# Crossing from one token tile to the next at the junctions of a two-layer trunk, and 13 adaLN steps moved into its first turns

## The chip, the cores and the metric

The kernel runs on one core of one Trainium2 chip. The metric is the device time of one execution in microseconds (us). Engines: PE (TensorE, matmuls), DVE (VectorE), ACT (ScalarE), POOL (GpSimd), SP (SyncE, which here only issues DMAs).

## The reference

Two layers act on 256 tokens of width 2048, in float32. Each layer is a token mixer and an MLP, both between norms that a conditioning vector modulates (adaLN):

```python
def reference(x, c, ...):
    cs = jax.nn.silu(c)
    for l in range(DEPTH):
        mod = (cs @ ada_w[l] + ada_b[l])[:, None, :]
        sh_a, sc_a, g_a, sh_m, sc_m, g_m = jnp.split(mod, 6, axis=-1)
        h = rms_norm(x, norm_g[l, 0]) * (1.0 + sc_a) + sh_a
        o = fox_sb_mixer(h, ...) if l % 2 == 0 else dsa_mixer(h, ...)
        x = x + g_a * rms_norm(o @ mix_w_out[l], norm_g[l, 1])
        h = rms_norm(x, norm_g[l, 2]) * (1.0 + sc_m) + sh_m
        y = jnp.square(jax.nn.relu(h @ ff_w1[l])) @ ff_w2[l]
        x = x + g_m * rms_norm(y, norm_g[l, 3])
    return x
```

`ada_w` is [2, 2048, 12288], `ff_w1` [2, 2048, 8192], `mix_w_out` [2, 2048, 2048]. A next norm needs a whole row of x, and that needs a whole row of the product before it: between `o @ mix_w_out` and `h @ ff_w1`, and between the MLP and the next layer's mixer, nothing of the next product can begin until every column of the last one is there.

## The kernel before, in words

**Tokens.** The 256 tokens are two tiles of 128 (t = 0, 1). X holds the residual, Y the branch, HT the normed and modulated activations, transposed, as two parts (high and low) of a split product.

**Weights.** Every weight matrix is cut into strips of columns and each strip into slots along the contraction. `order` lists all slots. A slot's weights are split on chip: ACT makes the high part (`wh`, L1261), DVE the low part (`wl`, L1265), `AHEAD` = 3 slots ahead of PE (`convert(s, 0)` and `convert(s, 1)`). There are four buffers each for `wh` and `wl`, so a conversion waits until PE is through with the slot four before. In each slot `mm_slot` issues the matmuls. In a "wmov" strip (both out-projections, the second MLP product, the mixer inputs) the weight moves and the tokens stand: three products per k and tile (L728 to L730). In a "wide" strip (the first MLP product) the weights stand and both tiles move: 512 columns of HT high and low together (L738) and 256 with `wl` (L740).

**Evictions.** At a strip's end its `evac` goes to `posts`; each slot runs one stage of it. `junction` is what stands behind the last strip of out_proj(0), MLP(0) and out_proj(1): it drains the posts, makes the statistics of both tiles together (`rstd_next`, with a power on POOL), writes the two diagonals DG (L420), transposes X by DG into HT two columns of 128 at a time (`ht_pair`: matmuls at L426, scale and shift on ACT at L437 and once on DVE at L435, cast L440, difference L441), and updates X (L467). The remaining pairs follow in `next_ht`, one pair per slot of the next strip. J1, J2 and J3 stand for these three junctions below.

**adaLN.** The product of silu(c) with `ada_w` runs on DVE in steps (`ada_step`, L296) of one [128, 1024] tile each, 512 KB by DMA through SP's queue; 16 steps make a job. Shift and scale of layer 0's first norm are wanted at once and come in 64 finer "parts" (`part_step`, L366) during four "turns" (the slots up to `phase_ends`: 3, 16, 32, 48), in which the first six weight units are multiplied by as much of HT as is there; HF holds HT's float copy. Later steps are paid from a balance, `owed`, that grows with each slot; a step is issued when it reaches 1. `attention_gate(0)`, called at slot GJ = 7 of the third strip of out_proj(0), first issues whatever steps are missing up to number 96 and then multiplies the gate into GG by a matmul with ones (L218).

The code stands in program order on every engine: no engine overtakes itself.

## Time and profile before

| | us |
|---|---|
| median of three runs | 2296.44 |
| the runs | 2292.89, 2296.44, 2297.43 |
| the profiled execution, whole | 2295.47 |
| its span, first to last instruction | 2293.6 |
| PE busy in the span | 2190.8 |
| DVE busy | 1684.9 |
| ACT busy | 1129.3 |
| mean granted clock of PE, as a share of full | 0.985 |

The profile is one execution; its times are read against its own 2295.47 us, of which 1.9 us lie outside the span. A row of a timeline says when an instruction (or a run of like ones) starts, how long it takes, on which engine and line, and in brackets how long the engine had been idle and what ended that. A busy PE need not be at full rate: the clock column of the windows says what was granted.

### The profile page before, as it was taken

How to read it: one execution, taken by the hardware profiler on the slowest of the kernel's cores; microseconds unless marked ns; L12 is line 12 of the kernel's file. 1: busy time of each engine (PE TensorE's matmuls, PEld its weight loads, DVE VectorE, ACT ScalarE, POOL GpSimd, SP SyncE). 2: the span in 40 equal slices, each digit the busy share in tenths (PEclk: the TensorE clock that was granted, in tenths of full speed). 3: DMA queues.
4: the chain of work that ended last, by engine and by line, in shares of the span. 5: the costliest groups of instructions: out<-in, count | busy, mean ns of one | idle time of the engine just before them, and what ended most of it. 6: DMA issues, size and time to landing. Idle time of an engine off the chain costs nothing. (4 is left out here: it accounts for less than half of the span.)

```text
span 2293.6 us, 30535 instructions
## 1 busy us (share of the span) xinstructions
PE 2190.8 (96%) x11750; PEld 1869.3 (81%) x11750; DVE 1684.9 (73%) x2085; ACT 1129.3 (49%) x1675; POOL 69.6 (3%) x97
## 2 busy tenths in 40 slices
PE   5899999958999999999999999999999999999998
PEld 3787898747888888888888878888888888888887
DVE  5777888867988998898888777656655655655655
ACT  1322466626554643643555546656544543643553
POOL 1000001100000000000000000000000000000000
PEclk9999999979999999999999999999999999999999
DMA  9997988865999999899898344454766766666564
GB/s 342 330 319 267 326 305 303 316 233 170 335 339 362 331 353 340 315 351 339 298 331 294 122 149 163 153 174 160 252 225 211 226 214 221 209 231 205 180 202 129
DMA packets 273618, 592.23 MB, mean 258 GB/s; under 512 B 13462, under 2 KB 46378, under 8 KB 272704
## 3 DMA queue, kind: packets, MB, share of 16 engines
q1 hardware_dynamic: 272000, 585.95, 74.6%
q0 software_dynamic: 1472, 4.33, 0.6%
q8 instruction: 92, 1.51, 0.3%
q14 instruction: 54, 0.44, 0.1%
HBM read 588.13 MB, written 2.10 MB: 257 GB/s over the span
## 5 line engine op out<-in xcount | busy, mean ns | idle before, releaser
L1261 ACT ACTIVATE wh<-wraw 128x1024 fp32r<-128x1024 f32 (+1 forms) x712 | 740.8, 1045 | 869.2 <-PE bank L730 470.9
L1265 DVE TENSOR_TENSOR wl<-wraw,wh 128x1024 fp32r<-128x1024 f32 (+1 forms) x712 | 852.5, 1205 | 257.2 <-ACT wh L1261 256.6
L738 PE MATMUL bank<-HT,wh 128*128 128x512 f32 x2048 | 716.0, 392 | 0.4 <-DVE HT L441 0.4
L740 PE MATMUL bank<-HT,wl 128*128 128x256 f32 x2048 | 578.9, 283 | 1.2 <-DVE wl L1265 1.2
L728 PE MATMUL bank<-wh,OT 128*128 128x512 f32 (+1 forms) x1408 | 529.8, 376 | 0.0
L730 PE MATMUL bank<-wh,OT 128*128 128x512 f32 (+1 forms) x1408 | 523.4, 372 | 0.0
L729 PE MATMUL bank<-wl,OT 128*128 128x512 f32 (+1 forms) x1408 | 519.4, 369 | 0.0
L738 PEld LDWEIGHTS bank<-HT,wh 128*128 128x128 f32 x2048 | 385.5, 188 | 81.7 <-DVE HT L441 1.0
L296 DVE SCALAR_TENSOR_TENSOR acc<-adat,CS,acc 128x1024 f32<-128x1024 f32 x320 | 410.5, 1283 | 52.3 <-DMA adat<-in_ada_w_dram 51.1
L740 PEld LDWEIGHTS bank<-HT,wl 128*128 128x128 f32 x2048 | 388.0, 189 | 3.9 <-DVE wl L1265 3.1
L730 PEld LDWEIGHTS bank<-wh,OT 128*128 128x128 f32 x1408 | 264.4, 188 | 50.2
L729 PEld LDWEIGHTS bank<-wl,OT 128*128 128x128 f32 x1408 | 264.7, 188 | 48.4 <-issue 1.2
L728 PEld LDWEIGHTS bank<-wh,OT 128*128 128x128 f32 x1408 | 265.0, 188 | 43.9 <-issue 0.8
L747 PE MATMUL bank<-HT,wh 128*128 128x256 f32 x448 | 129.1, 288 | 0.0
L751 PE MATMUL bank<-HT,wl 128*128 128x256 f32 x448 | 125.2, 279 | 1.5 <-DVE wl L1265 1.4
L728 PE MATMUL bank<-wh,HT 128*128 128x512 f32 (+2 forms) x320 | 123.5, 386 | 2.7 <-ACT wh L1261 1.4
L749 PE MATMUL bank<-HT,wh 128*128 128x256 f32 x448 | 125.2, 279 | 0.0
L729 PE MATMUL bank<-wl,HT 128*128 128x512 f32 (+2 forms) x320 | 118.8, 371 | 2.9 <-DVE wl L1265 2.9
L730 PE MATMUL bank<-wh,HT 128*128 128x512 f32 (+2 forms) x320 | 118.3, 370 | 0.0
L1005 DVE TENSOR_TENSOR ring<-bank,ring 128x256 f32<-128x256 f32 x128 | 51.3, 422 | 51.5 <-ACT ring L1004 48.6
L751 PEld LDWEIGHTS bank<-HT,wl 128*128 128x128 f32 x448 | 84.2, 188 | 2.0 <-DVE wl L1265 2.0
L747 PEld LDWEIGHTS bank<-HT,wh 128*128 128x128 f32 x448 | 84.2, 188 | 1.7 <-issue 1.6
(238 smaller groups left out, 1703.5 us busy)
## 6 DMA issues: line engine op xcount, KB each, us to landing
wraw<-in_ff_w_dram SPq DMA_DIRECT2D x256, 1024.0 KB, 6.3
adat<-in_ada_w_dram SPq DMA_DIRECT2D x338, 512.0 KB, 6.2
wraw<-in_even_w_in_dram SPq DMA_DIRECT2D x37, 1024.0 KB, 7.1
wraw<-in_mix_w_out_dram SPq DMA_DIRECT2D x32, 1024.0 KB, 5.6
wraw<-in_odd_w_in_dram SPq DMA_DIRECT2D x24, 1024.0 KB, 5.2
eb<-in_ada_w_dram SPq DMA_DIRECT2D x24, 512.0 KB, 6.2
wraw<-in_even_w_in_dram SPq DMA_DIRECT2D x12, 688.0 KB, 6.1
eb<-in_ada_w_dram SPq DMA_DIRECT2D x16, 256.0 KB, 7.8
```

What stands on the lines that cost most here:

```text
L296: nc.vector.scalar_tensor_tensor(acc, t, CS[:, j:j + 1], acc, ALU.mult, ALU.add)
L728: nc.tensor.matmul(o, src[:, k, 0, ts], wh[:, i, 0:w], start=first and i == 0, stop=False)
L729: nc.tensor.matmul(o, src[:, k, 0, ts], wl[:, i, 0:w], start=False, stop=False)
L730: nc.tensor.matmul(o, src[:, k, 1, ts], wh[:, i, 0:w], start=False, stop=last and i == len(ks) - 1)
L738: nc.tensor.matmul(o, wh[:, i, bs], src[:, k].rearrange("p a s -> p (a s)"), start=first and i == 0, stop=False)
L740: nc.tensor.matmul(o[:, S:], wl[:, i, bs], src[:, k, 0, :], start=False, stop=last and i == len(ks) - 1)
L747: nc.tensor.matmul(o, wh[:, i, bs], src[:, k, 0, :], start=first and i == 0 and b % 2 == 0, stop=False, skip_group_check=True)
L749: nc.tensor.matmul(o, wh[:, i, bs], src[:, k, 1, :], start=False, stop=False, skip_group_check=True)
L751: nc.tensor.matmul(o, wl[:, i, bs], src[:, k, 0, :], start=False, stop=last and i == len(ks) - 1, skip_group_check=True)
L1005: nc.vector.tensor_tensor(a[:, b], ps[:, 0:S], a[:, b], ALU.add)
L1261: nc.scalar.activation(wh[:, :, 0:w], r, AF.Copy)
L1265: nc.vector.tensor_sub(wl[:, :, 0:w], r, wh[:, :, 0:w])
```

## The change

Three things are done.

**Memory and early loads.** HF shrinks from 16 to 8 columns of 128 (k taken modulo 8), the room becomes two more `eb` tiles, and the part accumulators live there. The three `adat` buffers hold only parts 0 to 7; later parts rotate over five buffers in place of eight. So the normal steps' first three tiles can be loaded at the end of the first turn.

**Steps in the third and fourth turn.** In each of the turns 3 and 4, `owed` grows by RX = 0.65 in ten slots. 13 steps of the normal adaLN thus stand among the parts there.

**Junctions by one tile at a time.** `cross` takes the place of the `flush` code. The last strip before a junction (256 columns, four slots) runs tile 0 alone, and its tile-1 matmuls are kept in `rest`; no conversion is issued in its later slots. Then, in program order: statistics and DG of tile 0, the tile-1 matmuls with two conversions (`feed`) between, the first transposes of tile 0 (`ht_quad`, four columns of one tile at once), statistics of tile 1, two more conversions, four fresh slots of the next strip on tile 0 alone, the transposes of tile 1. The main loop then runs these four slots on tile 1. In a wide strip the 512 moving columns become twice 256. The other quads follow in `next_ht`, at slots 0 to 3, each x_update right in front of the quad that wants it.

```diff
+RX = 0.65
-            return (ep.tile([P, KC, S], F32, name="HF"),
-                    [ep.tile([P, 1024], F32, name=f"eb{i}") for i in range(4)])
+            return (ep.tile([P, 8, S], F32, name="HF"),
+                    [ep.tile([P, 1024], F32, name=f"eb{i}") for i in range(6)])
...
-            acc = acp.tile([P, 1024], F32, name="acc", tag="acc")
+            acc = q_accs[max(p - 1, 0) % 2]
...
-            t = q_bufs[i % len(q_bufs)]
+            t = q_bufs[i if i < 8 else (i - 8) % 5]
...
+        def ht_quad(t, k4, phase, fast=False):
             ps = aux()
             ps = [ps, aux()] if fast else [ps, ps]
+            for i in range(4):
+                k = 4 * k4 + i
+                nc.tensor.matmul(ps[i % 2][:, i * P:(i + 1) * P], X[:, t, k * P:(k + 1) * P], DG[:, t],
+                                 start=True, stop=True)
+            tmp = ring()
+            for i in range(4):
...
+                if fast and i % 2:
+                    nc.vector.tensor_scalar(dst, src, gs, sh, ALU.mult, ALU.add)
+                else:
+                    nc.scalar.activation(dst, src, AF.Identity, scale=gs, bias=sh)
...
+            nc.vector.tensor_copy(HT[:, ch, 0, ts], t3)
+            nc.vector.tensor_sub(HT[:, ch, 1, ts], t3, HT[:, ch, 0, ts])
...
             def f(j):
-                if 2 + j < 8:
-                    ht_pair(2 + j, phase)
-                    if j in (0, 2):
-                        for t in range(NT):
-                            x_update(t, j * 256 + 1024, 512)
-                else:
+                if j in (0, 2):
+                    for t in range(NT):
+                        x_update(t, j * 256 + 1024, 512)
+                if j < 4:
+                    ht_quad(j % 2, 2 + j // 2, phase)
+                if j >= 6:
...
+        def cross(s, st, rest):
+            phase, ready = st.skew
+            while posts:
+                post()
+            ready()
+            g = st.evac(st)
+
+            def normed(t):
+                rstd_next(t)
+                diag_rstd((t,))
+                x_update(t, 0, 512)
+                x_update(t, 512, 512)
+
+            next(g)
+            normed(0)
+            for i, (ks, wh, wl) in enumerate(rest):
+                mm_slot(st, ks, wh, wl, [1])
+                if i < 2:
+                    feed(s + 1 + i)
+            ht_quad(0, 0, phase, True)
+            next(g)
+            feed(s + 3)
+            ht_quad(0, 1, phase)
+            normed(1)
+            for _ in g:
+                pass
+            st.release()
+            gate_on[0] = False
+            feed(s + 4)
+            for i in range(s + 1, s + 5):
+                st, q = plan[order[i][0]]
+                j = 2 * q + order[i][1]
+                mm_slot(st, range(j * st.kper, (j + 1) * st.kper), *convs[i], [0])
+            ht_quad(1, 0, phase)
+            ht_quad(1, 1, phase)
...
+            hold = st.skew and j > 0
+            if s + AHEAD < nslots and order[s + AHEAD][0] in raws and not hold:
+                feed(s + AHEAD, 0)
...
+            if st.fresh and j < 4:
+                mm_slot(st, ks, wh, wl, [1])
...
-                    if p == 3:
-                        ada_ahead(6 * KC)
...
+                if s + 1 == phase_ends[0]:
+                    ada_ahead(6 * KC)
+                if p >= 2 and 1 <= r < 11:
+                    owed += RX
```

Two places are shown as they stand in the programs. On DVE, in front of the gate of out_proj(0) (in the kernel before L296 is an adaLN step, L1265 a `wl`, L220 the gate's multiplication, L928 the late multiplication of a stored strip):

```order
L296 SCALAR_TENSOR_TENSOR acc<-adat,CS,acc 128x1024
L1265 TENSOR_TENSOR wl<-wraw,wh 128x1024
L296 SCALAR_TENSOR_TENSOR acc<-adat,CS,acc 128x1024
L1265 TENSOR_TENSOR wl<-wraw,wh 128x1024
L296 SCALAR_TENSOR_TENSOR acc<-adat,CS,acc 128x1024 x13
L220 TENSOR_TENSOR QK<-bank_84,QK 128x512
L220 TENSOR_TENSOR QK<-bank_81,QK 128x512
L220 TENSOR_TENSOR QK<-bank_85,QK 128x512
L220 TENSOR_TENSOR QK<-bank_88,QK 128x512
L928 TENSOR_TENSOR Y<-Y,QK 128x512
```

The same place in the changed kernel, where L299, L1323, L223 and L952 are those lines:

```order
L299 SCALAR_TENSOR_TENSOR acc<-adat,CS,acc 128x1024
L1323 TENSOR_TENSOR wl<-wraw,wh 128x1024
L299 SCALAR_TENSOR_TENSOR acc<-adat,CS,acc 128x1024
L1323 TENSOR_TENSOR wl<-wraw,wh 128x1024
L223 TENSOR_TENSOR QK<-bank_88,QK 128x512
L223 TENSOR_TENSOR QK<-bank_84,QK 128x512
L223 TENSOR_TENSOR QK<-bank_81,QK 128x512
L223 TENSOR_TENSOR QK<-bank_87,QK 128x512
L952 TENSOR_TENSOR Y<-Y,QK 128x512
```

The run of 13 steps is gone: at the gate all 96 have been issued, and 13 more than before stand among the parts of turns 3 and 4.

On ACT, across J1 in the kernel before (L401 squares of a bank or of Y, L420 the diagonals, L437 scale and shift of the transposed columns, L1261 a `wh`):

```order
L401 ACTIVATE JUNKA,ST<-bank_84 128x256
L401 ACTIVATE JUNKA,ST<-Y 128x256
L401 ACTIVATE JUNKA,ST<-bank_81 128x256
L401 ACTIVATE JUNKA,ST<-Y 128x256
L420 ACTIVATE DG<-ident,RS 128x128 x2
L437 ACTIVATE ring<-bank_85,MV 128x256
L437 ACTIVATE ring<-bank_86,MV 128x256 x2
L1261 ACTIVATE wh<-wraw 128x1024
```

And in the changed kernel (L409, L428, L463 and L1319 are those lines):

```order
L409 ACTIVATE JUNKA,ST<-bank_88 128x256
L409 ACTIVATE JUNKA,ST<-Y 128x256
L428 ACTIVATE DG<-ident,RS 128x128
L1319 ACTIVATE wh<-wraw 128x1024 x2
L463 ACTIVATE ring<-bank_81,MV 128x128 x2
L409 ACTIVATE JUNKA,ST<-bank_84 128x256
L409 ACTIVATE JUNKA,ST<-Y 128x256
L1319 ACTIVATE wh<-wraw 128x1024
L463 ACTIVATE ring<-bank_85,MV 128x128 x4
L428 ACTIVATE DG<-ident,RS 128x128
L1319 ACTIVATE wh<-wraw 128x1024
L463 ACTIVATE ring<-bank_87,MV 128x128 x4
```

Tile 1's squares and a conversion stand between the first and the second quad of tile 0, and tile 1's diagonal stands in front of the fourth fresh slot's conversion.

On DVE, at the same place of the changed kernel, from the first quad's end (L466 the cast, L467 the difference, L963 the gated Y of tile 1, L496 to L514 statistics, L486 the update of X):

```order
L466 CAST HT<-ring 128x4x128
L467 TENSOR_TENSOR HT<-ring,HT 128x4x128
L963 TENSOR_TENSOR Y<-bank_84,QK 128x256
L496 TENSOR_REDUCE red<-ST 128x1
L405 TENSOR_SCALAR ms<-red 128x1
L423 SCALAR_TENSOR_TENSOR JUNKV,ST<-X,Y 128x256
L1323 TENSOR_TENSOR wl<-wraw,wh 128x1024
L466 CAST HT<-ring 128x4x128
L467 TENSOR_TENSOR HT<-ring,HT 128x4x128
L509 TENSOR_REDUCE red_4136<-ST 128x2
L510 TENSOR_SCALAR red_4136<-red_4136 128x1
L513 TENSOR_SCALAR sq<-red_4136,RS 128x1
```

Tile 1's gated Y stands behind the first quad's difference, and tile 1's statistics behind the second's.

## Rows read from the trace of the kernel before

**Rows 1.** Page, part 1: busy us (share of the span) xinstructions of each engine.

```profile
PE 2190.8 (96%) x11750; PEld 1869.3 (81%) x11750; DVE 1684.9 (73%) x2085; ACT 1129.3 (49%) x1675; POOL 69.6 (3%) x97
```

**Rows 2.** Waits of PE: waiter <- awaited: us in total, times, longest us.

```profile
PE bank L426 <- ACT DG L420: 32.6, 4, 14.4
PE bank L218 <- DVE acc L296: 23.2, 1, 23.2
```

**Rows 3.** Timeline of PE, gate: start us, us, engine line op [idle before].

```profile
470.49 1.88 PE L218 MATMUL bank<-acc,ones 128*128 128x512 f32 x4
495.60 3.78 PE L218 MATMUL bank<-acc,ones 128*128 128x512 f32 x4 [23.23 <-DVE acc L296]
498.39 1.20 PE L728 MATMUL bank<-wh,OT 128*128 128x256 f32 x1
```

**Rows 4.** Groups of DVE, 470.5 to 495.7: busy us, mean ns | idle before.

```profile
L296 DVE SCALAR_TENSOR_TENSOR acc<-adat,CS,acc 128x1024 f32<-128x1024 f32 x12 | 15.4, 1285 | 10.4 <-DMA adat<-in_ada_w_dram 10.1
```

**Rows 5.** Timeline of the SP queue at the gate.

```profile
469.75 19.77 SPq L197 DMA_DIRECT2D adat<-in_ada_w_dram  x10
```

**Rows 6.** Windows: us, busy (xinstructions) by engine, clock, DMA share, GB/s.

```profile
460.00:470.00 10.00, 10.00 (x45) 8.22 (x44) 8.37 (x7) 3.94 (x4) 0.00 (x0) 1.00 1.06 375
480.00:490.00 10.00, 0.00 (x0) 0.00 (x0) 6.44 (x6) 0.00 (x0) 0.00 (x0) 0.50 0.83 270
500.00:510.00 10.00, 10.00 (x87) 10.00 (x86) 9.86 (x18) 6.83 (x12) 0.00 (x0) 0.99 0.38 109
```

**Rows 7.** Windows of the third turn and of the fourth.

```profile
97.00:142.00 45.00, 43.19 (x233) 34.51 (x231) 31.46 (x34) 11.12 (x17) 0.00 (x0) 1.00 0.88 300
142.00:191.00 49.00, 47.54 (x273) 40.70 (x273) 37.34 (x46) 10.51 (x14) 1.58 (x2) 0.97 0.81 276
```

**Rows 8.** Timeline of all engines across the third junction.

```profile
1560.12 0.74 POOL L398 TENSOR_TENSOR RS<-ms,BQ 128x2 f32<-128x2 f32 x1 [76.81 <-DVE ms L397]
...
1561.83 1.41 DVE L467 SCALAR_TENSOR_TENSOR X<-Y,RS,X 128x512 f32<-128x512 f32 x2
1562.07 1.05 POOL L498 TENSOR_TENSOR RS<-sq,BQ 128x2 f32<-128x2 f32 x1 [1.20 <-DVE sq L497]
...
1563.15 0.69 ACT L420 ACTIVATE DG<-ident,RS 128x128 f32<-128x128 f32 x2 [2.92 <-POOL RS L498]
...
1563.61 3.79 PE L426 MATMUL bank<-DG,X 128*128 128x128 f32 x16 [5.04 <-ACT DG L420]
...
1564.87 0.56 ACT L437 ACTIVATE ring<-bank,MV 128x256 f32<-128x256 f32 x1 [1.02 <-PE bank L426]
...
1566.37 0.43 DVE L440 CAST HT<-ring 128x512 fp32r<-128x512 f32 x1
...
1566.84 0.69 DVE L441 TENSOR_TENSOR HT<-ring,HT 128x512 fp32r<-128x512 f32 x1
...
1567.59 0.80 PE L738 MATMUL bank<-HT,wh 128*128 128x512 f32 x1 [0.20 <-DVE HT L441]
...
1568.34 1.05 ACT L1261 ACTIVATE wh<-wraw 128x1024 fp32r<-128x1024 f32 x1
...
1570.88 1.22 DVE L1265 TENSOR_TENSOR wl<-wraw,wh 128x1024 fp32r<-128x1024 f32 x1
1570.90 1.05 PE L426 MATMUL bank<-DG,X 128*128 128x128 f32 x8
```

**Rows 9.** Timeline of PE at the first and the second junction.

```profile
530.44 3.79 PE L426 MATMUL bank<-DG,X 128*128 128x128 f32 x16 [8.04 <-ACT DG L420]
...
1265.16 3.47 PE L426 MATMUL bank<-DG,X 128*128 128x128 f32 x16 [5.12 <-ACT DG L420]
```

**Rows 10.** Timeline of PE after the first turns.

```profile
208.03 0.39 PE L728 MATMUL bank<-wh,HT 128*128 128x344 f32 x1 [1.32 <-DVE Y L799]
209.14 0.42 PE L729 MATMUL bank<-wl,HT 128*128 128x344 f32 x1 [0.72 <-DVE wl L1265]
```

**Rows 11.** Windows of that place.

```profile
210.00:213.00 3.00, 3.00 (x13) 3.00 (x12) 3.00 (x6) 1.01 (x1) 0.00 (x0) 0.50 0.71 242
```

More of the change, by code (lines that the diff above doesn't have):

```diff
@@ L416, in out_stats, with diag_rstd @@
                                            accum_out=ST[:, 2, t, n:n + 1])
-        def diag_rstd():
-            for t in range(NT):
+        def diag_rstd(tiles=range(NT)):
+            for t in tiles:
                 nc.scalar.activation(DG[:, t], ident, AF.Copy, scale=RS[:, 1, t:t + 1])
@@ L736, in mm_slot @@
                     bs = slice(b * P, (b + 1) * P)
+                    if len(tiles) == 1:
+                        ts = slice(tiles[0] * P, (tiles[0] + 1) * P)
+                        for i, k in enumerate(ks):
+                            nc.tensor.matmul(o.rearrange("p (a s) -> p a s", s=S)[:, :, ts], wh[:, i, bs], src[:, k, :, ts],
+                                             start=first and i == 0 and tiles[0] == 0, stop=False, skip_group_check=True)
+                            if tiles[0] == 1:
+                                nc.tensor.matmul(o[:, S:], wl[:, i, bs], src[:, k, 0, :], start=False, stop=False,
+                                                 skip_group_check=True)
+                        continue
                     for i, k in enumerate(ks):
                         nc.tensor.matmul(o, wh[:, i, bs], src[:, k].rearrange("p a s -> p (a s)"),
-                                         start=first and i == 0, stop=False)
+                                         start=first and i == 0, stop=False, skip_group_check=st.fresh)
                         nc.tensor.matmul(o[:, S:], wl[:, i, bs], src[:, k, 0, :], start=False,
-                                         stop=last and i == len(ks) - 1)
+                                         stop=last and i == len(ks) - 1, skip_group_check=st.fresh)
             else:
@@ L767, in f @@
             def f(j):
-                if 2 + j < 8:
-                    ht_pair(2 + j, phase)
-                    if j in (0, 2):
-                        for t in range(NT):
-                            x_update(t, j * 256 + 1024, 512)
-                else:
+                if j in (0, 2):
[4 more added lines that the diff above has]
+                if j >= 6:
                     x_sums(2 * j - 12)
@@ L948, in junction, with ready @@
         def junction(phase, need, limit):
-            def f():
+            def ready():
                 drain()
                 mixed.clear()
-                gate_on[0] = False
                 ada_ensure(need)
                 ada_ahead(limit * KC)
-                rstd_next()
-                diag_rstd()
-                ht_pair(0, phase, True)
-                ht_pair(1, phase)
-                for t in range(NT):
-                    x_update(t, 512, 512)
-            return f
+            return phase, ready
+        def cross(s, st, rest):
[31 more added lines that the diff above has]
+            ht_quad(1, 1, phase)
         def out_proj(l, phase, ada, adv):
@@ L990, in out_proj @@
                 add(st)
-            sts[-1].flush = True
             sts[-1].on_slot = x_square
-            sts[-1].after = junction(phase, *((5, 18) if l == 0 else (17, 20)))
+            sts[-1].skew = junction(phase, *((5, 18) if l == 0 else (17, 20)))
         out_proj(0, 1, RA0, 1)
@@ L1052, in mlp @@
                 for n, (c0, w) in enumerate(cols):
+                    end = q == 3 and n == len(cols) - 1
                     st = Strip(ff_w2[l], q * 2048, c0, w, "wmov", None, ev_w2(l, q, n), ada=ada,
-                               after=after if q == 3 and n == len(cols) - 1 else None)
+                               after=after if end and l == 1 else None, skew=after if end and l == 0 else None)
                     if l == 0 and q == 0 and n == 0:
@@ L1267, in convert, with feed @@
                 load_raw(i + 3)
+        made = set()
+        def feed(s, part=None):
+            for a in (0, 1) if part is None else (part,):
+                if (s, a) not in made:
+                    made.add((s, a))
+                    convert(s, a)
         for i in range(3):
@@ L1295, in body @@
             st, q = plan[i]
-            if s + AHEAD < nslots and order[s + AHEAD][0] in raws:
-                convert(s + AHEAD, 0)
             j = 2 * q + half
+            hold = st.skew and j > 0
+            if s + AHEAD < nslots and order[s + AHEAD][0] in raws and not hold:
+                feed(s + AHEAD, 0)
             if s + 1 in phase_ends:
@@ L1308, in body @@
             ks = range(j * st.kper, (j + 1) * st.kper)
-            if s < nslots - 4:
+            if st.fresh and j < 4:
+                mm_slot(st, ks, wh, wl, [1])
+            elif s < nslots - 4 and not st.skew:
                 mm_slot(st, ks, wh, wl)
@@ L1354, in body @@
                 st.release()
-            if st.done == KC:
+            if st.done == KC and st.skew:
+                if st.need is not None:
+                    ada_ensure(st.need)
+                cross(s, st, rest)
+                rest.clear()
+            elif st.done == KC:
                 if st.need is not None:
@@ L1376, in body @@
                         post()
-            if s + AHEAD not in convs:
-                convert(s + AHEAD, 0)
-            convert(s + AHEAD, 1)
+            if not hold:
+                feed(s + AHEAD)
 _INS = ['x', 'c', 'positions', 'ada_w', 'ada_b', 'norm_g', 'mix_w_out', 'even_w_in',
```

76 lines of the change are left out of this document (39 added, 37 removed).

## The prediction

> **What bounds the kernel now.** I read the page first: PE is busy for 96% of the span [rows 1], so time can only be won or lost where PE stands still or runs at its low clock. The table of PE's waits says where. Two waits hold most of it: one of 23.2 us for an adaLN accumulator, and four for a diagonal, 32.6 us together [rows 2]; 14.4 of these are the start of the program, which the change leaves as it is, and the three others are J1, J2 and J3 with 8.04, 5.12 and 5.04 us [rows 8, 9]. Next I read the timeline at the long wait: PE has the first half of the gate's matmuls at 470.49, then idles 23.23 us until 495.60 [rows 3]. DVE has 12 steps to do there, 15.4 us of work, and waits 10.4 us between them for their tiles [rows 4], because ten loads stand on SP's queue from 469.75 for 19.77 us [rows 5], at a DMA share of 0.83 [rows 6]. Last I read every engine across J3 [rows 8], since the new crossing is made of the same instructions.
>
> **The change part by part.**
>
> *The gate, -25.4.* The 13 steps in a row are gone, so the second half of the gate's matmuls follows the first. The first took 1.88 us, so both end near 470.49 + 3.76 = 474.25; the next strip began at 498.39, that is 24.2 later. Its first matmul took 1.20 at the low clock, and a few more ran slow [rows 3]; in the window after, 87 matmuls take 10 us, 0.115 each [rows 6]. That is another 1.2. What is late next? The slot's own `wl` and the loads. In the 10 us before the gate the DMA engines are full, at a share of 1.06 and 375 GB/s [rows 6], yet PE is never short of weights there, and the change takes 13 tiles of 512 KB away at or before this place and adds none. So I keep 25.4, with 24 as its lower end and, if the loads are late again (a rival), down to 0.
>
> *The turns, +1.5.* 13 steps of 1.285 us [rows 4] come in, 6 in the third turn and 7 in the fourth: 7.7 and 9.0 us of DVE. DVE idles there for 45 - 31.5 = 13.5 and 49 - 37.3 = 11.7 us [rows 7]. So they fit on the average. But the steps stand in front of the `wl` of the same slots, and DVE has no idle time in some 20 us of the fourth turn, where a step pushes each later `wl`. Walking the fourth turn with a step of 1.285 at its places, one `wl` ends 0.9 us after PE wants it; in the third I find 0 to 1. Their 13 loads (6.8 MB) want 20 us at the 300 GB/s of that stretch, with a DMA share of 0.88 and 0.81 [rows 7], so 94 us have about 14 us of unused share; that is short by some 6 us if nothing else gives way. Five buffers in place of eight shorten the parts' lead. So 0 if all hides, +6 if the DMA queue does not; I take +1.5, near the DVE walk, as PE already has 96 to 97% of both windows and its waits are at the turns' ends. If DVE's cover is gone, each step costs up to its 1.285.
>
> *The junctions before.* What does one lose against a PE that never stops? At J3 PE idles 5.04; the first transposes start at 1563.61 and the first fresh matmul at 1567.59, 3.98 later, where 16 records of 128 columns at full clock would take about 1.9 (8 take 1.05 [rows 8]); then 0.9 more, since the first fresh matmuls run low (0.80). Sum 8.0. With the same 3.0 behind each wait J1 loses 8.04 + 3.0 = 11.0 and J2 5.12 + 3.0 = 8.1. All three: 27.1.
>
> *The crossing at J3 now.* I walk it with the durations of J3, counting from the end of tile 0's matmuls. The rest on tile 1 is 4 slots of 12 matmuls at 0.115 to 0.1175: it ends at 5.6. Tile 0's diagonal: before, DG began at 1563.15, 4.6 after PE's end (1563.61 - 5.04 = 1558.57) for both tiles; with one tile POOL's 1.05 and the small steps shrink, about 4.1. So the diagonal is hidden, and the old wait goes. The new waits:
> - First quad: transposes 5.6 to 7.5 (two quads, 0.9 each); its scale and shift, on ACT and DVE side by side, to 7.5; then DVE, which still has the two `wl` of 1.22 in front, cast 0.43, difference 0.69: 9.6. PE waits 2.1 from 7.5.
> - Two fresh half slots, 0.94 each (8 times 256 columns), to 11.5. The third wants the second quad. On ACT its four pieces (0.34 each, from the two diagonals' 0.69) stand behind the squares of tile 1, where the square of Y waits until DVE has finished the first difference at 9.6, and behind a conversion of 1.05: pieces end at 13.1, cast and difference 14.1. PE waits 2.6.
> - The fourth wants its `wh`, which ACT makes behind tile 1's diagonal: DVE's statistics stand behind the difference at 14.1, five small steps, POOL 0.8, diagonal at 16.3, conversion 17.4. PE waits 2.3.
> - Tile 1's transposes 18.3 to 20.2, then 1.4 for four pieces, cast and difference, 22.2: PE waits 2.0.
> - In the main loop each x_update pair (1.41) now stands right in front of its quad, and behind the cast and difference of the one before; the quad of slot 2 starts at 32.7, 3.0 late. Small waits: 0.3.
> Together 12.3, and 0.2 for splitting 512 columns into twice 256, and 0.2 for the conversions behind: 12.7 at full clock. J3 was 8.0, so +4.7.
>
> *J2* goes into a wmov strip: its third and fourth slot need `wl` as well, and the same walk gives waits of 2.3, 2.3, 3.2, 2.1, 0.7 and 3.6: 14.2 against 8.1, +6.1. *J1* is J3 with the evictions of two strips still in line when tile 0 ends, so its diagonal comes 2.5 later: 15.2 against 11.0, +4.2. The sum is +15.0.
>
> *The clock.* After gaps of 1.32 and 0.72 us [rows 10] the clock is 0.50 for all of 210 to 213 [rows 11]: the low level of 1.2 GHz, for 3 us and more. The crossing has five gaps of 2 to 3 us within 25 us, so I expect low clock through much of it. A matmul that waits anyway may be slow for nothing; walking with the PE times doubled, the waits shrink (12.5 to 7.9) but the whole loses 15.3, +2.6 to +3.0. Bounds: 0, if the full clock stays or the gaps hide it all, and 9 for three times the 3.0 (more is rival B). I take +5.5 for the three: crossings +20.5, and 10 to 27 as its ends.
> The Trainium skill's page "TensorE: Matmul & The Clock Gate", in "A second HAM failure mode: psum-queue depth-cycling", warns that PE idling for moments between groups of matmuls makes the clock swing and costs throughput; by that the doubled walk holds, as rows 10 and 11 bear out for one place. The page's section "HAM oscillation — how this bites in real kernels" has a rule by which only longer gaps than these lower the clock; by it the 5.5 would be 0 and the time 2286.6, but rows 10 and 11 stand against it.
>
> *Sum.* -25.4 + 1.5 + 20.5 = -3.4. From the profiled execution's 2295.5 that is 2292.1, or 4.3 below the median of the runs, 2296.4, itself 0.9 above the profiled run. What a measurement of this kernel can tell from no change is about 0.2%, 4.6 us: the forecast lies at that edge, as no more than a small gain.
>
> **The rivals.**
>
> *A. The crossing is no dearer than the junction was (faster, 2270 to 2283).* For it: the old waits of 18.2 us for diagonals go in full, and a walk of row durations may put one queue behind another where PE is in truth held by neither; the second and third waits hang on ACT's order alone. Against it: each new wait stands behind work that rows time, and DVE and ACT do nothing less. If the crossings lose what the junctions lost, the time is 2295.5 - 25.4 + 1.5 = 2271.6; halfway, 2282.
>
> *B. The crossing's chain of hand-offs at the low clock (slower).* One mechanism, at the crossings: each quad goes PE, ACT, DVE, PE, and at the low clock transposes and half slots take twice as long while `wl`, cast, difference and x_update stand in one DVE line. From +8.5 a crossing on (sum +25) the gate's gain is spent; if no wait shrinks, PE's own work of 3.6 us of transposes and 3.8 of half slots adds 7.4 when doubled, each crossing costs some +12, and the sum is -25.4 + 1.5 + 36 = +12, 2307.6. For it: rows 10 and 11. Against it: PE's slow matmuls lie partly under waits.
>
> *C. The stall at the gate comes back elsewhere.* If 13 loads do not fit into the turns, where the unused DMA share is 14 us against 20 wanted, DVE waits on a tile in front of a `wl`, and 6 to 20 us return in turns 3 and 4 or at the gate: 2298 to 2312. Against it: the loads start up to 370 us before the gate, at 470.
>
> *D. The change doesn't do what it says*, i.e. the 13 steps are issued elsewhere but the second half of the gate still waits. In the programs' order they are gone, so this has next to no chance.
>
> **How the numbers follow.** The forecast, with crossings between +15 and +25, gives 2287 to 2297 and has 0.46 (0.24 of it faster than the edge, 0.22 within 0.2%). A has 0.22, all faster. B has 0.23: 0.08 within and 0.15 slower. C has 0.08: 0.03 within and 0.05 slower. D 0.01, within. So faster 0.46, same 0.34, slower 0.20. The range that leaves 2 in 10 outside runs from 2276, inside A, to 2304, inside B; the forecast's own is 2287 to 2297.
>
> **What would show it.** Right: no wait of the gate's matmuls (L223 in the changed kernel) for an accumulator; at each crossing PE's waits before a transpose for the diagonal gone or under 1 us, and in their place some five of 2 to 3 us, for HT (L467), for `wh` or `wl`, and for X (L486) at the third main-loop slot; a clock of 0.50 in windows of each crossing; J2 the dearest against before. In the fourth turn one or two waits for `wl` of 1 us at most. Wrong: waits at the crossings of under 1.5 us each (A); a granted clock at the low level through all 35 us of a crossing (B); DVE waiting on `adat` or on a part's tile for more than 3 us in the turns, or an accumulator wait at the gate again (C). If the gate gives less than 24, the first step of this working fails.

## The result: 25 us slower, and the profile after

The changed kernel took 2321.75 us (median of 4 runs, 2317.94 to 2323.83) against 2296.3 us before (4 runs): a ratio of 1.0111, 95% interval 1.0099 to 1.0123. The forecast was 2292.1, with a range from 2276 to 2304, so the prediction was wrong. The profiled execution of the changed kernel is the run of 2317.94 us, with a span of 2316.2; it is 3.8 us below the median, so what follows accounts for 22.6 of the 25.5 us.

First the page, part 1, PE's share of the changed kernel, as in [rows 1]:

```profile
PE 2205.2 (95%) x11814; PEld 1882.4 (81%) x11814; DVE 1690.7 (73%) x2103; ACT 1139.0 (49%) x1720; POOL 74.4 (3%) x103
```

The table of PE's waits of the changed kernel, longest sums first (waiter <- awaited: us in total, times, longest us):

```profile
PE bank L387 <- DVE eb L371: 15.0, 4, 6.3
PE bank L434 <- ACT DG L428: 14.4, 1, 14.4
PE bank L453 <- DVE X L486: 9.9, 4, 3.3
PE bank L755 <- DVE HT L467: 9.3, 4, 3.3
PE bank L743 <- ACT wh L1319: 6.4, 3, 2.4
```

The two big entries of [rows 2] are gone: there is no wait of the gate's matmuls (now L221), and of the waits for the diagonal only the program's start is left in this list (one of 2.1 us, at J1, stands further down the table, where the prediction wanted under 1). In their place stand waits of 2 to 3 us for X, HT and `wh`. But for that one the trace so far does what the prediction said. The 15.0 us at L387, the column sums of the parts in the turns, were 10.7 before.

To see where the time went, the same places of the program are set side by side: the last column sum of the fourth turn, the strip behind the gate, and the last strip (256 columns) before J2, before J3 and at the program's end. The timeline of PE in the kernel before:

```profile
190.53 1.95 PE L379 MATMUL bank<-ones,acc 128*128 128x1 f32 x16 [0.73 <-DVE acc L366]
...
1237.26 0.28 PE L728 MATMUL bank<-wh,OT 128*128 128x256 f32 x1
...
1535.79 0.28 PE L728 MATMUL bank<-wh,OT 128*128 128x256 f32 x1
...
2262.42 0.28 PE L728 MATMUL bank<-wh,OT 128*128 128x256 f32 x1
```

And in the changed kernel, with the gate between:

```profile
207.91 1.95 PE L387 MATMUL bank<-ones,eb 128*128 128x1 f32 x16 [2.52 <-DVE eb L371]
...
493.72 3.59 PE L221 MATMUL bank<-acc,ones 128*128 128x512 f32 x8
496.75 0.68 PE L743 MATMUL bank<-wh,OT 128*128 128x256 f32 x1
...
1241.94 0.28 PE L743 MATMUL bank<-wh,OT 128*128 128x256 f32 x1
...
1550.47 0.28 PE L743 MATMUL bank<-wh,OT 128*128 128x256 f32 x1
...
2285.01 0.28 PE L743 MATMUL bank<-wh,OT 128*128 128x256 f32 x1
```

The lag of the changed kernel, its start of a place less that of the kernel before, is 17.4 us at the end of the turns (207.91 - 190.53), 23.2 where the gate begins (493.72 against 470.49 in [rows 3]), -1.6 at the strip behind the gate (496.75 against 498.39), +4.7 before J2, +14.7 before J3 and +22.6 at the end. So the turns and the stretch up to the gate lost 23 us, the gate gave 25 back, and the three crossings cost 6.3, 10.0 and 7.9 us.

One execution of each kernel was profiled, so the spread has to be known. The kernel before and the eight runs below whose turns are as in it (e2, e5, e6, e7, e9, e12, e13, e14) have the last column sum between 188.23 and 193.79; the changed kernel and the three with its turns (e1, e8, e10) have it between 206.03 and 208.95. The lag of the turns is far outside that spread. The start of the strip behind the gate is not: 496.12 to 502.40 for before, e2, e5, e6, e7 and e9, and 496.75 to 499.85 for the changed kernel, e1, e8 and e10. So up to there the moved steps won nothing that can be told from zero.

### The profile page after: what moved, and what is told of

The parts are those of the page before. It is cut to its first block, busy times and chain, and to the rows that moved or that the text cites. A ratio compares the mean times of both kernels' runs of the same rounds, so it can differ in the third digit from the quotient of the medians.

```text
span 2316.2 us, 30729 instructions
## 1 busy us (share of the span) xinstructions
PE 2205.2 (95%) x11814; PEld 1882.4 (81%) x11814; DVE 1690.7 (73%) x2103; ACT 1139.0 (49%) x1720; POOL 74.4 (3%) x103
## 5 line engine op out<-in xcount | busy, mean ns | idle before, releaser
L1319 ACT ACTIVATE wh<-wraw 128x1024 fp32r<-128x1024 f32 (+1 forms) x712 | 740.8, 1045 | 877.9 <-PE bank L745 463.8
L1323 DVE TENSOR_TENSOR wl<-wraw,wh 128x1024 fp32r<-128x1024 f32 (+1 forms) x712 | 852.8, 1206 | 272.1 <-ACT wh L1319 271.4
L762 PE MATMUL bank<-HT,wh 128*128 128x512 f32 x1984 | 691.3, 391 | 0.0
L764 PE MATMUL bank<-HT,wl 128*128 128x256 f32 x1984 | 560.1, 282 | 0.0
L762 PEld LDWEIGHTS bank<-HT,wh 128*128 128x128 f32 x1984 | 373.3, 188 | 78.5 <-ACT wh L1319 0.5
L299 DVE SCALAR_TENSOR_TENSOR acc<-adat,CS,acc 128x1024 f32<-128x1024 f32 x320 | 410.9, 1284 | 30.4 <-DMA adat<-in_ada_w_dram 29.9
L764 PEld LDWEIGHTS bank<-HT,wl 128*128 128x128 f32 x1984 | 375.8, 189 | 0.8 <-issue 0.5
L775 PE MATMUL bank<-HT,wl 128*128 128x256 f32 x448 | 125.7, 281 | 3.2 <-DVE wl L1323 3.1
L771 PEld LDWEIGHTS bank<-HT,wh 128*128 128x128 f32 x448 | 84.5, 189 | 4.1 <-ACT wh L1319 2.7
L775 PEld LDWEIGHTS bank<-HT,wl 128*128 128x128 f32 x448 | 84.3, 188 | 4.2 <-DVE wl L1323 4.2
```

Source lines behind the costliest of these rows:

```text
L299: nc.vector.scalar_tensor_tensor(acc, t, CS[:, j:j + 1], acc, ALU.mult, ALU.add)
L762: nc.tensor.matmul(o, wh[:, i, bs], src[:, k].rearrange("p a s -> p (a s)"), start=first and i == 0, stop=False, skip_group_check=st.fresh)
L764: nc.tensor.matmul(o[:, S:], wl[:, i, bs], src[:, k, 0, :], start=False, stop=last and i == len(ks) - 1, skip_group_check=st.fresh)
L771: nc.tensor.matmul(o, wh[:, i, bs], src[:, k, 0, :], start=first and i == 0 and b % 2 == 0, stop=False, skip_group_check=True)
L775: nc.tensor.matmul(o, wl[:, i, bs], src[:, k, 0, :], start=False, stop=last and i == len(ks) - 1, skip_group_check=True)
L1319: nc.scalar.activation(wh[:, :, 0:w], r, AF.Copy)
```

## What the turns show

Windows of the changed kernel, its third turn and its fourth, cut at the same distance from the column sums as those of [rows 7] (columns as in [rows 6]):

```profile
102.26:151.30 49.04, 45.10 (x236) 35.91 (x234) 40.03 (x42) 11.12 (x17) 1.28 (x2) 0.97 0.94 330
```

```profile
151.30:208.40 57.10, 50.30 (x273) 42.44 (x273) 45.65 (x53) 10.90 (x15) 0.00 (x0) 0.94 0.88 315
```

Against [rows 7] the DMA share has risen from 0.88 and 0.81 to 0.94 and 0.88. The third turn has grown from 45.0 to 49.0 us and the fourth from 49.0 to 57.1; the other 5.3 us were lost before: the column sum at the second turn's end starts at 94.95, and at 89.69 in the kernel before. In the fourth turn PE idles 6.8 us, 1.5 before, and the same 273 matmuls take 2.8 us longer, at a clock of 0.94 against 0.97. What the DMA engines moved in the two turns, in the kernel before (97 to 191) and then in the changed one (102.26 to 208.4):

```profile
DMA packets 14991, 27.04 MB, mean 288 GB/s; under 512 B 735, under 2 KB 4831, under 8 KB 14986
```

```profile
DMA packets 17328, 34.20 MB, mean 322 GB/s; under 512 B 990, under 2 KB 5086, under 8 KB 17321
```

7.2 MB more, of which the 13 tiles are 6.8. The timeline of ACT near the end of the fourth turn shows who waits for them, in the kernel before and then in the changed one:

```profile
176.34 2.00 ACT L1261 ACTIVATE wh<-wraw 128x1024 fp32r<-128x1024 f32 x2 [15.02 <-DMA wraw<-in_even_w_in_dram]
187.59 2.11 ACT L1261 ACTIVATE wh<-wraw 128x688 fp32r<-128x688 f32 x3 [9.25 <-DMA wraw<-in_even_w_in_dram]
```

```profile
192.33 2.00 ACT L1319 ACTIVATE wh<-wraw 128x1024 fp32r<-128x1024 f32 x2 [19.34 <-DMA wraw<-in_even_w_in_dram]
204.98 2.11 ACT L1319 ACTIVATE wh<-wraw 128x688 fp32r<-128x688 f32 x3 [10.64 <-DMA wraw<-in_even_w_in_dram]
```

The weights come late: ACT stands 19.34 and 10.64 us for a `wraw` tile, where it stood 15.02 and 9.25 before. In the two turns its waits for `wraw` add up to 58.3 us, against 41.1. The two waits shown do not end for the same reason. Windows of the end of the fourth turn before, of the changed kernel up to its first wait's end, and two rows of its SP queue:

```profile
175.00:191.00 16.00, 15.27 (x81) 10.53 (x79) 11.03 (x11) 4.11 (x5) 0.00 (x0) 1.00 0.49 155
```

```profile
168.00:193.00 25.00, 23.10 (x118) 17.83 (x116) 21.06 (x24) 2.68 (x3) 0.00 (x0) 1.00 1.04 393
```

```profile
189.13 8.28 SPq L200 DMA_DIRECT2D adat<-in_ada_w_dram  x2
197.50 11.54 SPq L1293 DMA_DIRECT2D wraw<-in_even_w_in_dram  x3
```

Before, 8 of the fourth turn's 9 us of unused share lie in its last 16 us, where the share is 0.49. In the changed kernel the engines are full (1.04) from 168 until the first weights are there. The second wait is one of the queue: of two tile loads from 189.13 on, one waits 7.5 us for its buffer, until a step has read it that itself stands behind the late `wl`, and the weights behind them are issued at 197.50 only; from 193 to 209 the share is 0.64. And the moved steps themselves wait for nothing. The group of DVE from 97 to 209, six steps in the third turn and seven in the fourth (busy us, mean ns | idle before):

```profile
L299 DVE SCALAR_TENSOR_TENSOR acc<-adat,CS,acc 128x1024 f32<-128x1024 f32 x13 | 16.7, 1281 | 0.0
```

## What the crossings show

The timeline of PE across J3 of the changed kernel, transposes and the slots that waited:

```profile
1573.19 1.95 PE L453 MATMUL bank<-DG,X 128*128 128x128 f32 x16
1577.54 2.11 PE L755 MATMUL bank<-HT,wh 128*128 128x256 f32 x16 [2.41 <-DVE HT L467]
1581.95 1.43 PE L755 MATMUL bank<-HT,wh 128*128 128x256 f32 x8 [2.30 <-DVE red L509]
1585.43 2.08 PE L755 MATMUL bank<-HT,wh 128*128 128x256 f32 x8 [2.06 <-ACT wh L1319]
1587.31 3.00 PE L453 MATMUL bank<-DG,X 128*128 128x128 f32 x16
1592.00 0.39 PE L755 MATMUL bank<-HT,wh 128*128 128x256 f32 x1 [1.69 <-DVE HT L467]
...
1602.70 1.63 PE L453 MATMUL bank<-DG,X 128*128 128x128 f32 x8 [2.85 <-DVE X L486]
```

The diagonal is not waited for any more (5.04 in [rows 8]). The walk had waits of 2.1, 2.6, 2.3, 2.0 and 3.0 us; measured are 2.41, 2.30, 2.06, 1.69 and 2.85, in the same order and at the same places. The transposes behind the third wait take 3.00 where those before it take 1.95: the clock has fallen. At J2 the waits stand at the same places. PE's timeline there shows the third slot waiting for HT, the fourth for `wh` and then for `wl`, and at the end the wait for X:

```profile
1273.26 0.50 PE L743 MATMUL bank<-wh,HT 128*128 128x512 f32 x1 [1.67 <-DVE HT L466]
1277.56 0.49 PE L743 MATMUL bank<-wh,HT 128*128 128x512 f32 x1 [2.39 <-ACT wh L1319]
1278.83 0.75 PE L744 MATMUL bank<-wl,HT 128*128 128x512 f32 x1 [0.77 <-DVE wl L1323]
...
1295.70 1.86 PE L453 MATMUL bank<-DG,X 128*128 128x128 f32 x8 [3.29 <-DVE X L486]
```

The walk of J2 had 2.3, 2.3, 3.2, 2.1, 0.7 and 3.6 us; measured are 1.75, 1.67, 3.16, 1.17, 0.86 and 3.29, smaller in sum (11.9 against 14.2).

## The experiments

Fourteen kernels ran, each against the kernel before on the same chip. Medians of before in the four groups were 2296.57 (e1 to e4), 2296.78 (e5 to e8), 2296.5 (e9 to e11) and 2294.72 (e12 to e14).

### The two parts alone: e1 and e2

e1 is the kernel before with the change's memory, `ada_ahead` and RX lines alone, the core of which is shown; e2 is the change with these lines as they were before.

```diff
+RX = 0.65
...
+        q_accs = eb[4:6]
...
+            t = q_bufs[i if i < 8 else (i - 8) % 5]
...
+                if s + 1 == phase_ends[0]:
+                    ada_ahead(6 * KC)
+                if p >= 2 and 1 <= r < 11:
+                    owed += RX
```

> The kernel before with only the adaLN part of the change (smaller HF, five rotating buffers, early loads, 13 steps moved), junctions as before. Theory 'bytes': up to the gate the DMA engines are the bound, so a tile moved to the front only pushes the weights behind it; the 23 us that the turns lose and the 25.4 us that the gate wins nearly cancel: 2293 to 2295 us, 1 to 3 below before. Rival 'gate gain is real, something in the crossing made the turns late': 2272 us.

> The kernel before with only the crossing, adaLN as before (the 13 steps in a row at the gate stand). If the crossings cost what the trace of the changed kernel shows (lag +6 to +7 at J1, +10.0 at J2, +7.9 at J3): 2296.3 + 24.5 = 2321 us, with PE's wait of 23 us at the gate still there. Rival 'crossings are near neutral and the rest of the loss comes from the adaLN part': 2300 us.

e1: 2293.88 us, ratio 0.9988 (0.9979 to 0.9996). e2: 2321.12 us, ratio 1.0104 (1.0088 to 1.0121). The adaLN part brings 2.7 us and not 24; the crossing alone costs 24.5. In e1 the timeline of PE at the gate:

```profile
495.24 3.60 PE L219 MATMUL bank<-acc,ones 128*128 128x512 f32 x8
498.27 0.68 PE L733 MATMUL bank<-wh,OT 128*128 128x256 f32 x1
```

The wait is gone and the strip behind the gate starts at 498.27, where it started at 498.39 before [rows 3]: what was waited there is now lost ahead of it.

### What makes the turns late: e3, e4, e11

All three are the changed kernel with one edit. e3 loads half of each of the first 13 tiles, and the step works on that half; the other half of this modulation is left out:

```diff
-            nc.sync.dma_start(t, src[:, j, :])
+            w = 512 if i < 13 else 1024
+            nc.sync.dma_start(t[:, 0:w], src[:, j, 0:w])
...
-            nc.vector.scalar_tensor_tensor(acc, t, CS[:, j:j + 1], acc, ALU.mult, ALU.add)
+            w = 512 if i < 13 else 1024
+            nc.vector.scalar_tensor_tensor(acc[:, 0:w], t[:, 0:w], CS[:, j:j + 1], acc[:, 0:w], ALU.mult, ALU.add)
```

e4 loads whole tiles, and the step works on an eighth, the rest being left out; e11 moves no step:

```diff
-            nc.vector.scalar_tensor_tensor(acc, t, CS[:, j:j + 1], acc, ALU.mult, ALU.add)
+            w = 128 if i < 13 else 1024
+            nc.vector.scalar_tensor_tensor(acc[:, 0:w], t[:, 0:w], CS[:, j:j + 1], acc[:, 0:w], ALU.mult, ALU.add)
```

```diff
-RX = 0.65
+RX = 0.0
```

> The changed kernel, but the first 13 adaLN tiles are loaded and multiplied in half their columns only (256 KB in place of 512; that part of the modulation is left out). Theory 'bytes': 3.4 MB less at some 340 GB/s is 10 us less lag at the end of the turns: 2311 to 2313 us. Rival 'queue': SP's queue is held by a load that waits for its buffer, whatever its size: 2321 us. Rival 'DVE': 13 steps shorter by 0.6 us each: 2319 us at best.

> The changed kernel with all loads whole, but DVE multiplies only 128 of the 1024 columns in the first 13 steps (the rest of that modulation is left out), so a step takes some 0.3 us. Theory 'bytes': the lag of the turns stays, 2320 to 2322 us. Rival 'DVE': the steps in front of the wl were what made the turns late, 13 times 1 us comes back: 2308 us. Rival 'queue' (buffers come free sooner): 2315 us.

> The changed kernel with RX = 0: no step in the turns, the three early tiles, the smaller HF and the five rotating buffers stay, the steps stand in a row at the gate again. Theory 'bytes': the turns lose only what three early tiles of 512 KB take, some 5 us at the end of the turns; the rest of the 17 us appears as a wait at the gate of some 18 us; the sum stays within 3 us of the changed kernel, 2319 to 2325. Rival 'the five buffers make the turns late': a lag of over 10 us at the end of the turns and the gate's wait besides, 2330 us or more.

e3: 2313.57 us, ratio 1.0077 (1.0064 to 1.009). e4: 2320.31, ratio 1.0099 (1.0083 to 1.0115). e11: 2323.75, ratio 1.0123 (1.0109 to 1.0137). The last column sum of the turns in e3, e4 and e11 (190.53 before, 207.91 in the changed kernel):

```profile
201.15 2.08 PE L389 MATMUL bank<-ones,eb 128*128 128x1 f32 x9 [3.20 <-DVE eb L373]
```

```profile
204.38 1.83 PE L388 MATMUL bank<-ones,eb 128*128 128x1 f32 x15 [0.82 <-DVE eb L372]
```

```profile
195.90 1.29 PE L387 MATMUL bank<-ones,eb 128*128 128x1 f32 x11
```

Of the 17.4 us, 5.4 stay without any moved step (e11); they come from the three tiles loaded early and the five buffers, which no run separates, and 4.8 of them are there at the second turn's end already (94.52 against 89.69). The 13 steps are 12.0. Half of their bytes (and half a step's time on DVE) is worth 6.8; their time on DVE, nearly all of it, 3.5, which is little beside the spread of these places: 204.38 is 1.7 below the lowest start of the kernels with the changed turns. So their loads are the larger part, and "DVE" alone is refuted, since 8.5 of the 12 stay with steps that are almost free. "Queue" is not refuted as a part: a tile's load that waits for its buffer holds SP's queue for up to 7.5 us in the fourth turn of the changed kernel and up to 8.1 in e3 and in e4, so none of these runs is without it.

e3's total came out 0.6 above what "bytes" had, in part by luck: the turns gave back 6.8 us and not 10, and of the 6.2 by which its profiled execution is shorter than the changed kernel's, 3.2 are there at the gate (490.55 against 493.72) and the rest comes at the crossings, which the edit does not touch. Not as expected: in e11 the gate's wait was 23.2 us, not 18, so the strip behind it starts at 500.99, 2.6 later than before. Between the last column sum and the gate PE idles 12.9 us in the changed kernel, 12.7 in e3 and 8.7 before; e3's matmuls there, 1720 in both, take 276.6 us against 272.9, at a clock of 0.97 against 0.98. Why that stretch idles more than before was not separated.

### The same 13 steps behind the turns: e12, e13, e14

e12 is the kernel before with one number changed; in e13 it is 1.12, and e14 is e12 with the fillers of e7 (below).

```diff
-        RA0 = 1.05
+        RA0 = 1.2
```

> The kernel before, nothing of the change, but the adaLN rate of the slots behind the turns is 1.2 in place of 1.05, so that the 13 steps of the row at the gate spread over the 280 us between the turns' end and the gate. Theory 'full queue in the turns only': there the DMA engines have some 30 us unused (shares of 0.76 to 0.94 in most windows) and DVE 50, so the gate's wait goes and little comes in its place: 2272 to 2282 us. Rival 'the DMA engines bound the whole way to the gate': the gate exit stays where it is and the weights come late instead: 2293 to 2297 us.

> The same with a rate of 1.12: seven steps stay in the row at the gate. Theory 'turns only': half of the gain, a wait of 11 to 13 us at the gate, 2283 to 2288 us. Rival: 2293 to 2297 us with a wait there of some 20.

> The rate of 1.2 and the fillers at the old junctions (2291.1 alone). If the gains add under 'turns only': 2267 to 2277 us; under the rival 2288 to 2291.

e12: 2281.85 us, ratio 0.9947 (0.9933 to 0.996). Timeline of PE at the gate of e12:

```profile
477.94 1.88 PE L218 MATMUL bank<-acc,ones 128*128 128x512 f32 x4
482.96 1.98 PE L218 MATMUL bank<-acc,ones 128*128 128x512 f32 x4 [3.15 <-DVE acc L296]
484.38 0.68 PE L728 MATMUL bank<-wh,OT 128*128 128x256 f32 x1
```

Its turns end as before, with the last column sum at 190.22. Its window of the stretch from there towards the gate:

```profile
191.00:470.00 279.00, 262.84 (x1680) 229.90 (x1680) 232.08 (x268) 151.17 (x243) 31.53 (x35) 0.99 0.90 320
```

The same 13 steps, paid behind the turns, cost PE 7.5 us on the way (477.94 against 470.49), leave a wait of 3.15 of the 23.23, and the strip behind the gate starts 14.0 earlier; the medians differ by 12.9. So the DMA engines do not bound the whole way to the gate; what ate the gain was the place in the turns, with the buffers given up for it. e13 did not come out as either theory: 2292.54, ratio 0.9992 (0.9979 to 1.0004), with a wait of 17.2 at the gate and the gate 10.3 late. Half the steps moved gave no half of the gain. Its profiled execution is the slowest of eleven (2299.64 us), so its places are no measure of the median; it does show what is left of the row, the group of DVE from 480.8 to 499.8:

```profile
L296 DVE SCALAR_TENSOR_TENSOR acc<-adat,CS,acc 128x1024 f32<-128x1024 f32 x9 | 11.5, 1283 | 8.4 <-DMA adat<-in_ada_w_dram 8.3
```

DVE still waits 8.3 us for the tiles of a shorter row, 10.1 in the full one [rows 4]. Why the gate comes 10.3 late was not separated. e14: 2278.16 us, ratio 0.9931 (0.9918 to 0.9943), 1.2 above its upper bound. It is the fastest kernel here, below both.

### The crossing's order and the clock: e5 to e10

e5 is e2 with n matmuls of 256 columns that nobody reads, in front of three fresh half slots, behind tile 1's transposes (14) and, in `next_ht`, in front of the late quad (20):

```diff
+        def fill(n):
+            if n:
+                ps = aux()
+            for _ in range(n):
+                nc.tensor.matmul(ps[:, 0:S], late["OT"][:, 0, 0, 0:P], late["OT"][:, 0, 0, :], start=True, stop=True)
...
+                fill({1: 17, 3: 18, 4: 16}.get(i - s, 0))
                 mm_slot(st, range(j * st.kper, (j + 1) * st.kper), *convs[i], [0])
             ht_quad(1, 0, phase)
             ht_quad(1, 1, phase)
+            fill(14)
...
+                if j == 2:
+                    fill(20)
```

e6 is e2 in another order, without fillers:

```diff
                 mm_slot(st, ks, wh, wl, [1])
+                feed(s + 1 + i, 0)
                 if i < 2:
-                    feed(s + 1 + i)
+                    feed(s + 1 + i, 1)
...
             ht_quad(1, 0, phase)
+            for t in range(NT):
+                x_update(t, 1024, 512)
             ht_quad(1, 1, phase)
...
-                if j in (0, 2):
-                    for t in range(NT):
-                        x_update(t, j * 256 + 1024, 512)
                 if j < 4:
                     ht_quad(j % 2, 2 + j // 2, phase)
+                if j == 0:
+                    for t in range(NT):
+                        x_update(t, 1536, 512)
```

> The kernel before with only the crossing, and matmuls that nobody reads (256 columns, 17, 18, 16, 14 and 20 of them) put on PE at the crossing's five places where it waits. Theory 'clock': PE then never stands still for long, keeps the high clock, and each crossing loses what the walk at full clock gives, 12.7 to 15 us, in place of the 16 to 18 measured: 2310 to 2313 us against 2321 with the bare crossing. Rival 'waits alone': the clock costs nothing because slow matmuls lie under waits; the fillers then only add, 2321 us or more.

> The kernel before with only the crossing, in another order: all four wh conversions directly behind the tile-1 matmuls that free their buffers, and each pair of x_updates one slot earlier than its quad. Theory 'the waits are the program order of ACT and DVE': by the walk of row durations at low clock a crossing loses 5.4 to 5.7 us less (15.3 to 9.9 at J3, 17.2 to 11.5 at J2), so 2304 to 2306 us against 2321. Rival 'the waits are the chain's own length, whatever the order': 2319 to 2321 us.

e5: 2312.2 us, ratio 1.0068 (1.0056 to 1.0081). e6: 2296.53 us, ratio 1.0004 (0.9995 to 1.0012). Windows across J3 in the changed kernel, in e5 and in e6:

```profile
1574.00:1609.00 35.00, 23.69 (x161) 22.45 (x160) 20.48 (x38) 16.41 (x40) 4.95 (x7) 0.85 0.30 100
```

```profile
1570.00:1605.00 35.00, 33.01 (x265) 31.70 (x264) 22.75 (x41) 19.41 (x43) 4.95 (x7) 1.00 0.34 110
```

```profile
1560.00:1590.00 30.00, 23.46 (x185) 22.22 (x184) 23.34 (x42) 19.71 (x43) 4.95 (x7) 1.00 0.44 139
```

With PE kept busy the clock stays at 1.00 at J3 (0.96 at J1, 1.00 at J2) and the three crossings cost 8.9 us less: that is what the low clock cost of the 24.5, as far as the fillers remove it. What is left, 15.4 us above the kernel before, is the crossing at full clock. At J3, from the last strip in front of it to the last strip of the program, the timeline of PE in e5:

```profile
1546.89 0.28 PE L737 MATMUL bank<-wh,OT 128*128 128x256 f32 x1
...
2278.37 0.28 PE L737 MATMUL bank<-wh,OT 128*128 128x256 f32 x1
```

That is 731.48 us where the kernel before takes 726.63, 4.9 more; the walk had +4.7. The other order keeps the clock at 1.00 at J3 too and takes all 24.6 back, 8 more than the walk gave, so that the crossing is worth what the old junction was. e6 makes two moves at once, the conversions and the x_updates, and no run separates them; nor is all of it the order alone, since the clock rises with it (at J1 and J2 it is 0.92 and 0.95 in e6). Its waits at J3, PE's timeline of e6:

```profile
1564.59 2.11 PE L749 MATMUL bank<-HT,wh 128*128 128x256 f32 x16 [2.84 <-DVE HT L461]
1567.95 2.13 PE L749 MATMUL bank<-HT,wh 128*128 128x256 f32 x16 [1.26 <-DVE HT L461]
...
1574.58 0.39 PE L749 MATMUL bank<-HT,wh 128*128 128x256 f32 x1 [1.93 <-DVE HT L461]
```

The waits for `wh` and for X are gone; that for HT is left.

e7 is the kernel before with fillers at its junctions, e8 the same on e1:

```diff
+                fill(60 if need == 5 else 38)
                 ht_pair(0, phase, True)
                 ht_pair(1, phase)
+                fill(10)
```

> The kernel before, junctions as they were, with 60 (J1) or 38 (J2, J3) matmuls that nobody reads on PE in front of the first transposes and 10 behind them. If the low clock behind each wait is what follows PE standing still, the transposes and first matmuls run at full clock and each junction loses some 2 us less: 2289 to 2292 us. Rival: the clock falls all the same, or the fillers run into the transposes: 2296 us or more.

> The adaLN part of the change (2293.9 alone) with the same fillers at the old junctions. If the two gains add: 2287 to 2290 us, below both kernels. Rival: 2294 us.

e7: 2291.1 us, ratio 0.9974 (0.9965 to 0.9983), as expected. The transposes of J3 in e7 run at full clock, 2.12 us where [rows 8] have 3.79:

```profile
1563.43 2.12 PE L426 MATMUL bank<-DG,X 128*128 128x128 f32 x16 [0.49 <-ACT DG L420]
```

e8: 2290.97, ratio 0.9973 (0.996 to 0.9986), 1.0 above its range: the adaLN part adds nothing that can be measured to the fillers.

e9 is e6, and e10 the changed kernel in e6's order, both with fillers in front of the first and third half slot and behind tile 1's transposes (12):

```diff
+                fill({1: 18, 3: 9}.get(i - s, 0))
                 mm_slot(st, range(j * st.kper, (j + 1) * st.kper), *convs[i], [0])
             ht_quad(1, 0, phase)
...
             ht_quad(1, 1, phase)
+            fill(12)
```

> The kernel before with the crossing in the second order (2296.5 without fillers) and matmuls that nobody reads at its three longest remaining waits (18, 9 and 12 of 256 columns). Theory 'clock': full clock through the crossing takes 2 to 3 us off each: 2288 to 2291 us. Rival 'waits alone': 2296 to 2299 us.

> The changed kernel with that order and those fillers. If the adaLN part brings the same 2.7 us as alone: 2285 to 2288 us, below both kernels and below the fillers at the old junctions (2291). If the adaLN part only trades places: as the run without it, 2288 to 2291.

e9: 2294.78 us, ratio 0.9992 (0.9983 to 1.0). A miss for "clock": at J3 the clock of e6 was 1.00 without fillers, so there was nothing to win there. At J1 the fillers took it from 0.92 to 0.96, at J2 it stayed at 0.95. e10: 2291.26, ratio 0.9978 (0.9969 to 0.9988), 3.5 below e9; its number was missed by 3 us, but it is the change with both faults of its crossing mended, and 30 us below the change as it was.

## Why the prediction was wrong, step by step

**The gate, -25.4: right in the trace.** The wait is gone and nothing else was late there; the lag changes by -24.8.

**The turns, +1.5 with 0 to +6: the step that failed.** They lost 17.4 by their end and 23.2 by the gate. The working had the figure in hand: 20 us of loads against 14 us of unused DMA share (at the 300 GB/s that it names, 6.8 MB take 22.7 us; 20 is what they take at the full share, 341). It took the DVE walk (0.9 us) as the nearer row and left the queue as an upper bound of 6, as if the unused share of a whole turn could be filled at any time. It could not: 8 of the fourth turn's 9 us lay in its last 16 us, and most of the tiles were loaded ahead of that. e11, e3 and e4 show 5.4 us for the three early tiles and buffers, and 12.0 for the 13 steps, mostly their loads. ACT waits 17.2 us more than before for weights while the steps wait 0.0 for their tiles: the tiles stand ahead of the weights in SP's queue. This is rival C (chance 0.08), whose short DMA share was right and whose price of 6 to 20 held for the turns and was too low for the whole way to the gate; its waiter was wrong, since it had DVE stand for a tile, and it was ACT that stood for weights. How much the full engines took and how much the held queue was not separated. e12 shows that the place was at fault and not the idea: the same steps behind the turns keep 14 of the 25 us at the gate.

**The crossings, +15.0 at full clock: right.** e5, at full clock, lies 15.4 above its kernel before. The five waits at J3 came out within 0.4 us each. The walk's total of 20.5 with the clock stands against 24.2 from the lags and 24.5 from e2.

**The clock, +5.5: too small, inside its bounds of 0 to 9.** e5 measures 8.9. In the changed kernel the clock falls to a mean of 0.85 over 35 us of J3, after waits of 2.41 and 2.30. The working had the waits shrink with a slow PE (12.5 to 7.9); in the trace the five at J3 add up to 11.3, near the 12.0 that the walk gave them at full clock. That slow matmuls came on top of the waits fits this, but was not tested.
The Trainium skill's page "TensorE: Matmul & The Clock Gate" has two rules here. By "A second HAM failure mode: psum-queue depth-cycling" short idles between groups of matmuls lower the clock; the trace of the changed kernel agrees (0.85 over 35 us). By "HAM oscillation — how this bites in real kernels" only longer gaps than these do; e6 at J3, with waits of 2.84 and 1.93 and a clock of 1.00, agrees with that; the changed kernel, with waits of 2.41 and 2.30 and a clock of 0.85, does not, and there the measurement decides.

**The sum.** -25.4 + 1.5 + 20.5 = -3.4 was forecast. Measured from the lags of one execution: +23.2 up to the gate, -24.8 at it, +24.2 at the crossings, +22.6 in all. Of the 26.0 us between the two sums 21.7 are the turns, 3.7 the crossings and 0.6 the gate.

## What to carry to other kernels

A transfer that is moved forward costs what it pushes back: look at what stands behind it in the same queue and whether an engine waits for that, and not at the mean unused share of the stretch. Here a walk and a byte count disagreed, and the larger one was nearer to the price. Cutting a hand-off chain with several engines into smaller pieces lost 24.5 us here, and writing the same pieces in another order on each engine's queue took them back, the low clock's share with them. Where a short wait can't be removed, matmuls that nobody reads can keep the clock up for the work behind it: 8.9 us in e5 and 5.7 in e7, though nothing clear in e9.

## What was not expected of the hardware

38 matmuls in an otherwise idle wait made the 16 transposes behind it take 2.12 us in place of 3.79, and three junctions together 5.7 us shorter. In e6 a wait of 2.84 us, with 1.26 and 1.93 behind it, left the clock at 1.00. In the changed kernel, with waits of 2.41, 2.30 and 2.06 behind one another, it was 0.57 from 1582 to 1590, the window's row:

```profile
1582.00:1590.00 8.00, 5.94 (x31) 5.64 (x32) 3.31 (x7) 2.09 (x5) 4.36 (x6) 0.57 0.28 61
```
